# Prompt value products in groups of eight score blocks, the sample's over pairs of page tiles

## The chip, the cores and the metric

The kernel runs on one core of one Trainium2 chip. The metric is the device time of one execution in microseconds (us). The engines are named as in the profile: PE is TensorE (matrix products), PEld its weight loads, DVE is VectorE, ACT ScalarE, POOL GpSimd, SP the engine that issues most transfers.

## The reference, cut to what matters

One inference step of a two-layer decoder for a prompt of 2048 tokens and for a sample batch of 8 sequences with 8 new tokens each, over 4096 cached positions. Layer one is a gated linear recurrence; layer two is attention with 16 heads of 64 over shared keys and values. Attention has a forgetting term, the difference of cumulative log forget values, and a causal mask. The sample's cached keys and values lie in pages of 128 positions, found through a page table.

```python
s = jnp.einsum('bqhd,bkhd->bhqk', q, k).astype(jnp.float32) * (HEAD_DIM ** -0.5)
s = s + jnp.swapaxes(cq, 1, 2)[:, :, :, None] - jnp.swapaxes(ck, 1, 2)[:, :, None, :]
s = jnp.where(mask[None, None], s, -jnp.inf)
p = jax.nn.softmax(s, axis=-1)
return jnp.einsum('bhqk,bkhd->bqhd', p.astype(v.dtype), v)
```

## The kernel before, in words

The recurrence layer comes first, in two chunks of the prompt, then the shared projections `k`, `v`, `q`, `g`, then prompt attention, then the output projection. The sample's attention (`decode`) is a generator that yields estimated costs; a `Side` object advances it beside the prompt's projections and attention, so the work of both stands mixed in the engines' programs. It works in 16 turns, one for a sequence and half of the heads; three turns run early (`ahead` false), the other thirteen beside the second half of the projections and beside attention (`ahead` true).

*Prompt attention* (`attention`). The work is cut into 64 units, a head and a query chunk `qc` of 512 columns; even heads go through `qc` 0 to 3, odd heads 3 to 0. A unit has 4(qc + 1) blocks of 128 keys, a head 40, all heads 640; one block is one tick. For a block, TensorE makes scores in one of two banks (`st`) with two matmuls (L1592 and L1593; on the diagonal a third, the causal mask, L1595). The contraction of 128 rows of the first holds the high and low parts of the keys (`ka`). ScalarE takes the exponential into a tile (L1601): block 0 of a unit into the unit's accumulator `acc`, the others into `p`, six buffers (NP). After every fourth block `product` is put off by two ticks. It issues the value products of the four blocks in one run with `together`: the first matmul waits for the last exponential, the others are ordered right behind it. Each product uses 64 of the 128 array columns (`ops`, L1612, `128*64`), two of them side by side for the two halves of the queries, and the trace holds two records for each. Then POOL adds the four tiles into `acc` (L108, a helper), and at the end of a unit `finish` copies the result (`oT`). After four units `total` sums the accumulators over keys (L1481), copies the sums to `cs` and stores them through SP.

The softmax maximum is a separate pass ahead of the scores: `top` makes a score block of queries against keys (`sx`, L1431) and VectorE reduces it. `advance` decides how many of these stand in each tick.

Keys and values of a head are loaded by `load_head` at the sixteenth tick of the head before: `ka`, two buffers of 2048 columns, in one transfer, and `vvt` (2048 positions by 64) in another. The low keys with the forget rows (`kbt`) and the queries have loads of their own. Loads are issued by SP, which works through its program in order; `paged` puts them behind the page load last written into the program.

*The sample* (`decode`). A page tile `raw` is four pages (128 positions by 8 heads by 64, 256 KB each) and is issued by SP (L1093). Beside attention there are four such buffers (`nraw`), taken in turn by key tiles, value tiles and two scratch tiles. A turn has eight key and eight value tiles. Key tiles are transposed on VectorE (`ktr`, L1180), which frees them, and four make a batch of scores (`dS`, L1148, `128*32`). For a value tile, `products` issues 8 matmuls, 16 records, in one run (`dO`, L1262, `128*32`, four side by side), as soon as the four pages have come; those of tile 0 are put off to the place of tile 1. The order of a period is written out by hand:

```python
for who, x in (("v", 5), ("k", 0), ("v", 6), ("k", 1), ("v", 7), ("k", 2), ("k", 3), ("v", 0), ("k", 4),
               ("v", 1), ("k", 5), ("v", 2), ("k", 6), ("v", 3), ("k", 7), ("v", 4)):
```

Here value tiles 5 to 7 belong to the turn before, and the key tiles to the next one.

*Output projection* (`project`). Seventeen row tiles, of which every other one uses lent tiles of attention: `kbt0`, one `ka` buffer (for two operands of 1024 columns) and one `vvt` tile for the output. The result of a row tile is stored whole, that of the last in halves.

Of the kernel before, what the change touches and what calls it, by code (L numbers as in the profile page):

```python
# [11 lines left out]
F32 = mybir.dt.float32  # L12
# [8 lines left out]
P = 128  # L21
# [35 lines left out]
NP = 6  # L57
# [30 lines left out]
def tile_hawk_fox(  # L88
# [954 lines left out]
    def decode(es, turns, nraw, nktr, ahead):  # L1043
# [74 lines left out]
        class Turn:  # L1118


            def __init__(self, it):
                self.b, self.hg, self.odd = *turns[it], it % 2
                self.next = turns[it + 1] if it + 1 < len(turns) else None
                self.dl, self.raws = Later(), []
# [125 lines left out]
        def values(t, xs):  # L1250
# [7 lines left out]
            def products(i, raw, came):  # L1258

                def mm(d, a):  # L1260
# [5 lines left out]
                together([partial(mm, d, a) for d in range(4) for a in range(2)], came, True)  # L1266
# [67 lines left out]
    def attention(es):  # L1334
# [46 lines left out]
        lent["psum"], lent["res"], lent["out"] = ps3, f(kbs[0][:, :]), vvs[0]  # L1381
        lent["halves"] = lambda: pool.tile([P, SEQ], F32R, name="ka", tag="ka", bufs=2)
        units = [(h, qc) for h in range(H) for qc in ((0, 1, 2, 3) if h % 2 == 0 else (3, 2, 1, 0))]
        heads, qas, mxs, oTs_, sgt = {}, {}, {}, {}, {}
# [17 lines left out]
        def load_head(h):  # L1402
            hr = slice(h * HD, (h + 1) * HD)
            ka = pool.tile([P, SEQ], F32R, name="ka", tag="ka", bufs=2)
            for lo, hi in halves(h):
                queue[0].dma_start(f(ka[:, lo:hi]), kd_d[h * HD:(h + 1) * HD, :, lo:hi].rearrange("d x t -> (d x) t"))
            queue[0].dma_start(vvs[h % 2][:, :, :], v_d[:, hr].rearrange("(k p) d -> p k d", p=P))
            heads[h] = ka
# [67 lines left out]
        def total(h2, sums, todo, single):  # L1476
# [5 lines left out]
            cs = pool.tile([P, 512], F32, name="cs", tag="cs")  # L1482
# [67 lines left out]
        load_head(0)  # L1550
# [6 lines left out]
        ops = acc = None  # L1557
        pair = []
# [10 lines left out]
        lows = [2]  # L1569

        def loads():
# [7 lines left out]
            h, k = divmod(tick, 40)  # L1579
            if k == 16 and h + 1 < H:  # L1580
                with paged():
                    load_head(h + 1)

        for u, (h, qc) in enumerate(units):
            for k in range(nks[u]):
                loads()
                ka, kb = heads[h], kbs[h % 2]
                qa, qb = qas[u], qbs[u % NQ]
                lo = max(0, k - qc * 4) * P
                ks = slice(k * P, (k + 1) * P)  # L1590
                ps = scores_bank()
# [309 lines left out]
```

## Time and profile before

| | |
|---|---|
| median of 3 runs | 3027.18 us (3025.36 to 3033.16) |
| the profiled execution's own time | 3028.43 us |
| its span, first to last instruction | 3026.4 us |
| mean granted TensorE clock | 0.969 |
| first value product of the sample beside the second half of the projections | 1404.3 us |
| first value product of the prompt | 1762.4 us |
| last value product of the sample | 2708.9 us |
| last value product of the prompt | 2823.7 us |

All places in the profile are microseconds from the start of the span. A row of the timeline has the start, the time until the end of the last instruction that it merges, engine, line, operation, tiles (output, then inputs), the array shape used, the shape of the moving operand and the number of merged records; an idle time before it stands in brackets with what ended it. Matmuls overlap in the pipeline, so the distance of two starts tells more than the length of one. A row of the waits has who waited for what, the total, the number of times and the longest.

### The profile page before, as it was taken

To read this page: it belongs to the slowest core of one execution; us is meant where nothing else is said; L and a number is where in the kernel's file an instruction comes from. 1 tells how busy PE (TensorE), PEld (TensorE's weight loads), DVE (VectorE), ACT (ScalarE), POOL (GpSimd) and SP (SyncE) were. 2 spreads that over 40 slices of the span, in tenths; PEclk is the share of its full clock that TensorE was granted. 3 is DMA by queue.
4 is the path that set the end of the run, shared out by engine and by line. 5 is a ranking of instruction groups with operands and counts; after the bars stand their busy time and mean duration, and the time that the engine had idled before them with its cause. 6 is when DMAs were issued, how large, how long until landed. Compare 5 with 4: busy or idle time off the path is not lost.

```text
span 3026.4 us, 60467 instructions
## 1 busy us (share of the span) xinstructions
PE 2803.4 (93%) x21614; PEld 2252.1 (74%) x21614; DVE 1805.5 (60%) x4012; ACT 1269.9 (42%) x2874; POOL 1084.4 (36%) x1199
## 2 busy tenths in 40 slices
PE   6998999998997999999999699998998999999998
PEld 5997789988887997888889556665665666565687
DVE  6877455425427775676564466656776756655344
ACT  4665342222125665534333234444544444355321
POOL 1653201000002653100000245665575656659422
PEclk9999999999998999999999889999999999999999
DMA  4224546888863226699999968898899888874343
GB/s 123 79 88 133 171 126 191 256 263 281 278 216 91 89 88 194 209 313 338 332 346 326 279 209 243 248 282 255 250 291 287 267 251 265 260 247 122 98 145 110
DMA packets 479103, 653.79 MB, mean 216 GB/s; under 512 B 91291, under 2 KB 277020, under 8 KB 471525
## 3 DMA queue, kind: packets, MB, share of 16 engines
q1 hardware_dynamic: 475174, 644.26, 67.4%
q10 hardware_dynamic: 3340, 3.56, 0.4%
q8 instruction: 171, 2.80, 0.4%
q0 software_dynamic: 288, 2.10, 0.2%
q14 instruction: 130, 1.06, 0.1%
HBM read 514.22 MB, written 135.16 MB: 215 GB/s over the span
## 4 chain that ended last, share of the span: by engine, by line
PE 59%; DMA 16%; DVE 9%; ACT 6%; SPq 5%; issue 3%; POOL 1%; ACTq 0%; DVEq 0%; POOLq 0%
PE ops L1612 7%; PE st L1592 4%; PE y L383 4%; PE y L384 4%; PE y L385 4%; DMA raw<-in_cache_k_dram 4%; PE sx L1431 4%; PE dO L1262 3%; DMA raw<-in_cache_v_dram 3%; PE st L1593 3%; PE dS L1148 3%; PE kv L383 3%; PE kv L385 3%; PE kv L384 3%; SPq L1093 2%
## 5 line engine op out<-in xcount | busy, mean ns | idle before, releaser
L108 POOL TENSOR_TENSOR acc<-acc,p 128x512 f32<-128x512 f32 (+3 forms) x576 | 640.9, 1114 | 347.7 <-PE ops L1612 211.2
L1601 ACT ACTIVATE p<-st 128x512 f32<-128x512 f32 (+3 forms) x576 | 291.3, 525 | 400.1 <-PE st L1593 177.5
L1180 DVE STREAM_TRANSPOSE ktr<-raw 128x1024 f32<-128x1024 f32 x256 | 308.2, 1226 | 125.1 <-DMA raw<-in_cache_k_dram 116.5
L1433 DVE TENSOR_REDUCE mxs<-sx 128x1 f32<-128x512 f32 x384 | 255.0, 681 | 141.0 <-PE sx L1431 139.6
L383 PE MATMUL kv<-wh,xh 128*128 128x256 f32 (+3 forms) x1088 | 310.0, 288 | 6.4 <-ACT wh L427 4.7
L384 PE MATMUL kv<-wl,xh 128*128 128x256 f32 (+3 forms) x1088 | 309.3, 287 | 5.7 <-DVE wl L428 5.7
L385 PE MATMUL kv<-wh,xl 128*128 128x256 f32 (+3 forms) x1088 | 309.6, 286 | 2.7 <-DMA xl<-xld 2.7
L1592 PE MATMUL st<-qa,ka 128*128 128x512 f32 (+3 forms) x640 | 269.9, 422 | 13.3 <-ACT p L1601 7.5
L1612 PE MATMUL ops<-p,vvt 128*64 128x256 f32 (+1 forms) x2176 | 262.9, 369 | 1.0 <-ACT p L1601 0.7
L1431 PE MATMUL sx<-kbt,qbt 96*128 96x512 f32 (+3 forms) x640 | 229.2, 416 | 29.9 <-DMA qbt<-qd 24.2
L1113 POOL TENSOR_TENSOR qw<-qb,amask 128x128 f32<-128x128 f32 x64 | 29.1, 460 | 618.1 <-PE dS L1148 325.3
L428 DVE SCALAR_TENSOR_TENSOR wl<-wst,gv,wh 128x256 fp32r<-128x256 f32 (+1 forms) x384 | 169.4, 504 | 131.8 <-ACT wh L427 131.5
L427 ACT ACTIVATE wh<-wst,gv 128x256 fp32r<-128x256 f32 (+1 forms) x384 | 164.6, 499 | 190.2 <-DMA wst<-in_w_kv_dram 72.7
L1593 PE MATMUL st<-qbt,kbt 128*128 128x512 f32 (+3 forms) x640 | 236.9, 370 | 0.0
L383 PE MATMUL qg<-xh,wh 128*128 128x512 f32 (+2 forms) x640 | 229.4, 359 | 0.0
L384 PE MATMUL qg<-xl,wh 128*128 128x512 f32 (+2 forms) x640 | 228.2, 357 | 0.0
L385 PE MATMUL qg<-xh,wl 128*128 128x512 f32 (+2 forms) x640 | 227.5, 356 | 0.6 <-DVE wl L428 0.6
L1612 PEld LDWEIGHTS ops<-p,vvt 128*64 128x64 f32 x2176 | 161.5, 141 | 88.2 <-issue 19.8
L383 PEld LDWEIGHTS kv<-wh,xh 128*128 128x128 f32 (+1 forms) x1088 | 203.5, 188 | 13.2 <-ACT wh L427 6.8
L384 PEld LDWEIGHTS kv<-wl,xh 128*128 128x128 f32 (+1 forms) x1088 | 203.2, 188 | 10.1 <-DVE wl L428 6.9
L385 PEld LDWEIGHTS kv<-wh,xl 128*128 128x128 f32 (+1 forms) x1088 | 204.8, 188 | 7.0 <-issue 3.7
L1592 PEld LDWEIGHTS st<-qa,ka 128*128 128x128 f32 x640 | 123.7, 193 | 112.8 <-issue 54.4
(297 smaller groups left out, 6356.3 us busy)
## 6 DMA issues: line engine op xcount, KB each, us to landing
raw<-in_cache_k_dram SPq DMA_DIRECT2D x512, 256.0 KB
raw<-in_cache_v_dram SPq DMA_DIRECT2D x512, 256.0 KB
wst<-in_w_kv_dram SPq DMA_DIRECT2D x48, 512.0 KB
wst<-in_b_w_in_dram SPq DMA_DIRECT2D x48, 512.0 KB
xt<-in_x_prompt_dram SPq DMA_DIRECT2D x32, 512.0 KB
wst<-in_a_w_in_dram SPq DMA_DIRECT2D x64, 256.0 KB
out_dram<-kf SPq DMA_DIRECT2D x128, 128.0 KB
sc<-cd SPq DMA_DIRECT2D x16, 1024.0 KB
```

The source lines that it names most:

```text
L108: eng.tensor_tensor(out, a, b, op=op)
L383: T.matmul(ps, lh(k), rh(k), start=(k == 0), stop=False)
L384: T.matmul(ps, lh(k), rl(k), start=False, stop=False)
L385: T.matmul(ps, ll(k), rh(k), start=False, stop=(k == nk - 1))
L428: V.scalar_tensor_tensor(wl[:, k, :], st[:, k, :], gk, f(wh[:, k, :]), op0=ALU.mult, op1=ALU.subtract)
L1180: behind("V", V.transpose(t.kts[pp][:, n], raw[:, :, pp * 256:(pp + 1) * 256]).ins)
L1431: T.matmul(ps[:, :w], qb[0:96, j * P:(j + 1) * P], kb[0:96, ck * 512:ck * 512 + w], start=True, stop=True)
L1433: place["V"] = V.reduce_max(mx[:, j, ck:ck + 1], ps[:, :w], axis=AX.X).ins
L1592: place["T"] = T.matmul(ps[:, lo:], ka[:, ks], qa[:, lo:], start=True, stop=False).ins
L1593: T.matmul(ps[:, lo:], kb[:, ks], qb[:, lo:], start=False, stop=(k < qc * 4))
L1601: pair.append((k, lo, p, A.activation(p[:, lo:], ps[:, lo:], AF.Exp)))
L1612: return T.matmul(ops[r * HD:(r + 1) * HD, a0 * P:], vvs[h % 2][:, k, :], p[:, :].rearrange("p (a r c) -> p a r c", a=2, r=2)[:, a0:, r, : ...
```

## The change

The prompt's value products of heads 0 to 14 are issued after every eighth block, for all eight blocks in one run, which may span two units; head 15 keeps groups of four. Block 0 goes into a `p` tile like the others, and there are ten of these. The additions into `acc` are issued right behind each exponential, the first one from blocks 0 and 1, and where block 1 covers only part of the columns POOL copies the rest from block 0. The row sums `cs` take a turn in the `p` ring and lose their own tile.

For the sample, in the thirteen later turns, the products of value tiles 0 and 1, 2 and 3, 4 and 5, 6 and 7 are issued in one run of 16 matmuls, which waits for the pages of both.

`ka` and `vvt` become three tiles each of half the length: one for the lower halves of even heads, one for those of odd heads, and one that the upper halves of all heads share. The lower halves are loaded 24 ticks ahead by SP, the upper ones early in their own head: for odd heads by ScalarE's queue, for even heads by SP.

In the output projection the lent tiles follow these halves, and each row tile's output is two tiles, stored separately.

```diff
-NP = 6
+NP = 10
+GROUP = 8
...
-            def products(i, raw, came):
-
-                def mm(d, a):
+            def products(pages_):
+
+                def mm(i, raw, d, a):
                     c = ((i + d) % 2 * 2 + a) * 32
                     return T.matmul(op[c:c + 32, :256], sx[:, d, i // 4, a * 4:(a + 1) * 4, :].rearrange("p h q -> p (h q)"),
                                     raw[:, d, a * 256:(a + 1) * 256],
                                     start=(i + d < 2), stop=(i + d == NPG - 1))
 
-                together([partial(mm, d, a) for d in range(4) for a in range(2)], came, True)
+                together([partial(mm, i, raw, d, a) for i, raw, _ in pages_ for d in range(4) for a in range(2)],
+                         [c for *_, came in pages_ for c in came], True)
...
-                dl.after(2 if ahead and x == 0 else 1, lambda i=x * 4, raw=raw, came=came: products(i, raw, came))
+                t.held.append((x * 4, raw, came))
+                if x % 2 or not ahead:
+                    dl.after(1, partial(products, t.held[:]))
+                    t.held.clear()
...
-        pool.tile([P, 512], F32, name="cs", tag="cs")
         pool.tile([P, 512], F32, name="sgt", tag="sgt", bufs=2)
-        vvs = [pool.tile([P, 16, HD], F32, name=f"vvt{i}") for i in range(2)]
-        pool.tile([P, SEQ], F32R, name="ka", tag="ka", bufs=2)
+        vvs = [pool.tile([P, 8, HD], F32, name=f"vvt{i}") for i in range(3)]
+        kas = [pool.tile([P, SEQ // 2], F32R, name=f"ka{i}") for i in range(3)]
...
-        def load_head(h):
-            hr = slice(h * HD, (h + 1) * HD)
-            ka = pool.tile([P, SEQ], F32R, name="ka", tag="ka", bufs=2)
-            for lo, hi in halves(h):
-                queue[0].dma_start(f(ka[:, lo:hi]), kd_d[h * HD:(h + 1) * HD, :, lo:hi].rearrange("d x t -> (d x) t"))
-            queue[0].dma_start(vvs[h % 2][:, :, :], v_d[:, hr].rearrange("(k p) d -> p k d", p=P))
-            heads[h] = ka
+        def place_of(h, k):
+            return h % 2 if k < 8 else 2
+
+        def load_ka(queue, h, k0, k1):
+            queue.dma_start(f(kas[place_of(h, k0)][:, k0 % 8 * P:((k1 - 1) % 8 + 1) * P]),
+                            kd_d[h * HD:(h + 1) * HD, :, k0 * P:k1 * P].rearrange("d x t -> (d x) t"))
+
+        def load_vv(queue, h, k0, k1):
+            queue.dma_start(vvs[place_of(h, k0)][:, k0 % 8:(k1 - 1) % 8 + 1, :],
+                            v_d[k0 * P:k1 * P, h * HD:(h + 1) * HD].rearrange("(k p) d -> p k d", p=P))
...
-            cs = pool.tile([P, 512], F32, name="cs", tag="cs")
+            cs = pool.tile([P, 512], F32, name="cs", tag="p", bufs=NP)
...
+        def products(todo):
+
+            def mm(u, k, lo, p, r):
+                h, qc = units[u]
+                a0 = (lo // P + 1 - r) // 2
+                return T.matmul(ops2[r * HD:(r + 1) * HD, u % 2 * 256 + a0 * P:u % 2 * 256 + 256],
+                                vvs[place_of(h, k)][:, k % 8, :],
+                                p[:, :].rearrange("p (a r c) -> p a r c", a=2, r=2)[:, a0:, r, :],
+                                start=(k == 0), stop=(k == nks[u] - 2 + r))
+
+            together([partial(mm, u, k, lo, p, r) for u, k, lo, p, _ in todo for r in range(2) if lo <= (2 + r) * P],
+                     [todo[-1][4]])
+            for u, k, *_ in todo:
+                if k == nks[u] - 1:
+                    finish(u, ops2[:, u % 2 * 256:u % 2 * 256 + 256], sums_of.pop(u))
...
+        lows, parts = [2], []
+        for h in range(1, H):
+            steps_ = [(-24, S, load_ka, 0, 8), (-24, S, load_vv, 0, 8)]
+            if h % 2:
+                steps_ += [(1, A, load_ka, 8, 12), (2, A, load_ka, 12, 16), (4, A, load_vv, 8, 16)]
+            else:
+                steps_ += [(4, S, load_ka, 8, 12), (5, S, load_vv, 8, 12), (10, S, load_ka, 12, 16), (11, S, load_vv, 12, 16)]
+            parts += [(h * 40 + t, q, fn, h, k0, k1) for t, q, fn, k0, k1 in steps_]
+        parts.sort(key=lambda x: x[0])
...
-            h, k = divmod(tick, 40)
-            if k == 16 and h + 1 < H:
-                with paged():
-                    load_head(h + 1)
+            while parts and tick >= parts[0][0]:
+                _, queue_, fn, *which = parts.pop(0)
+                with paged() if queue_ is S else ExitStack():
+                    fn(queue_, *which)
...
-                place["T"] = T.matmul(ps[:, lo:], ka[:, ks], qa[:, lo:], start=True, stop=False).ins
+                place["T"] = T.matmul(ps[:, lo:], ka[:, kx], qa[:, lo:], start=True, stop=False).ins
...
+                p = pool.tile([P, 512], F32, name="p", tag="p", bufs=NP)
+                group.append((u, k, lo, p, A.activation(p[:, lo:], ps[:, lo:], AF.Exp)))
                 if k == 0:
-                    p = acc = pool.tile([P, 512], F32, name="acc", tag="acc", bufs=NACC)
+                    first = p
+                elif k == 1:
+                    acc = sums_of[u] = pool.tile([P, 512], F32, name="acc", tag="acc", bufs=NACC)
+                    tt(a_l(), acc[:, lo:], first[:, lo:], p[:, lo:], ALU.add)
+                    if lo:
+                        cp(G, acc[:, :lo], first[:, :lo])
                 else:
-                    p = pool.tile([P, 512], F32, name="p", tag="p", bufs=NP)
-                pair.append((k, lo, p, A.activation(p[:, lo:], ps[:, lo:], AF.Exp)))
-
-                def product(u=u, h=h, todo=pair, acc=acc, last=(k == nks[u] - 1)):
-
-
-                    nonlocal ops
-                    if todo[0][0] == 0:
-                        ops = ops2[:, u % 2 * 256:u % 2 * 256 + 256]
-
-                    def mm(k, lo, p, r):
-                        a0 = (lo // P + 1 - r) // 2
-                        return T.matmul(ops[r * HD:(r + 1) * HD, a0 * P:], vvs[h % 2][:, k, :],
-                                        p[:, :].rearrange("p (a r c) -> p a r c", a=2, r=2)[:, a0:, r, :],
-                                        start=(k == 0), stop=(last and k == todo[-1][0] - 1 + r))
-
-                    together([partial(mm, k, lo, p, r) for k, lo, p, _ in todo for r in range(2) if lo <= (2 + r) * P],
-                             [todo[-1][3]])
-                    for k, lo, p, _ in todo:
-                        if k:
-                            tt(a_l(), acc[:, lo:], acc[:, lo:], p[:, lo:], ALU.add)
-                    if last:
-                        finish(u, ops, acc)
-
-                if k % 4 == 3:
-                    later.after(2, product)
-                    pair = []
+                    tt(a_l(), acc[:, lo:], acc[:, lo:], p[:, lo:], ALU.add)
+                if len(group) == (GROUP if h < H - 1 else 4):
+                    later.after(2, partial(products, group))
+                    group = []
...
-                V.scalar_tensor_tensor(y[:m, sl], yps[j][:m, :], r[:m, 0:1], bpostB[:m, sl], op0=ALU.mult, op1=ALU.mult)
-                tt(V if i == len(rows) - 1 and j == 1 else G, y[:m, sl], y[:m, sl], x1[:m, sl], ALU.add)
-                if i == len(rows) - 1:
-                    S.dma_start(dst[:, sl], y[:m, sl])
-            if i < len(rows) - 1:
-                S.dma_start(dst, y[:m, :])
+                V.scalar_tensor_tensor(y[j][:m, :], yps[j][:m, :], r[:m, 0:1], bpostB[:m, sl], op0=ALU.mult, op1=ALU.mult)
+                tt(V if i == len(rows) - 1 and j == 1 else G, y[j][:m, :], y[j][:m, :], x1[:m, sl], ALU.add)
+                S.dma_start(dst[:, sl], y[j][:m, :])
...
-                dict(og=tiled(lent["res"][:, :D]), x1=lent["res"][:, D:], oh=tiled(hs[:, :D]), ol=tiled(hs[:, D:]),
-                     y=lent["out"][:, :, :].rearrange("p k d -> p (k d)"),
+                dict(og=tiled(lent["res"][:, :D]), x1=lent["res"][:, D:], oh=tiled(lent["split"][0][:, :]),
+                     ol=tiled(lent["split"][1][:, :]), y=lent["out"],
```

More of the change, by code (lines that the diff above doesn't have):

```diff
@@ L1549, in attention @@
         advance(-1)
-        load_head(0)
+        for k in (0, 8):
+            load_ka(queue[0], 0, k, k + 8)
+            load_vv(queue[0], 0, k, k + 8)
         load_low(0)
@@ L1556, in attention @@
             yield 300
[L1557 to L1558 removed]
+        group, sums_of = [], {}
+        def products(todo):
[11 more added lines that the diff above has]
+                    finish(u, ops2[:, u % 2 * 256:u % 2 * 256 + 256], sums_of.pop(u))
         wide = [0]
```

16 lines of the change are left out of this document (7 added, 9 removed).

## The prediction

> **What bounds the kernel now.** I read the engine shares first, then the same shares by stage, then the waits of TensorE, then its timeline around single products.
>
> ```profile
> span 3026.4 us, 60467 instructions
> PE 2803.4 (93%) x21614; PEld 2252.1 (74%) x21614; DVE 1805.5 (60%) x4012; ACT 1269.9 (42%) x2874; POOL 1084.4 (36%) x1199
> ```
>
> TensorE leads. By stage (length, then busy time of PE, weight loads, DVE, ACT, POOL, then granted clock, DMA share, GB/s), for the three stages that the change touches:
>
> ```profile
> 1300.00:1730.00 430.00, 404.96 (x3725) 349.94 (x3723) 255.37 (x500) 153.77 (x397) 24.36 (x45) 0.98 0.99 328
> 1762.00:2710.00 948.00, 891.98 (x8168) 569.90 (x8167) 618.68 (x1311) 429.24 (x1063) 585.05 (x558) 0.97 0.84 260
> 2710.00:2826.00 116.00, 109.01 (x656) 68.11 (x655) 60.45 (x112) 69.14 (x147) 101.04 (x84) 1.00 0.40 118
> ```
>
> The first is shared projections with the sample beside them, the second prompt attention with the sample beside it, the third prompt attention alone. In each TensorE is busy 94% of the time, no other engine is (POOL comes near in the short third), and DMA is full only in the first. So a stretch of TensorE time that disappears should mostly shorten the run. What is in it?
>
> ```profile
> PEld st L1592 <- issue: 53.6, 166, 0.8
> PEld dO L1262 <- issue: 36.9, 57, 3.4
> PEld ops L1612 <- issue: 26.2, 95, 0.7
> PEld st L1592 <- ACT p L1601: 37.6, 87, 1.7
> PE st L1592 <- ACT p L1601: 7.5, 20, 0.8
> PEld ops L1612 <- ACT p L1601: 27.3, 64, 2.2
> PE ops L1612 <- ACT p L1601: 4.1, 7, 2.0
> PE dO L1262 <- DMA raw<-in_cache_v_dram: 19.4, 13, 3.1
> ```
>
> These are TensorE's waits in prompt attention (total us, times, longest). The first three name no releaser: the weight load sits idle without waiting for anything shown, and it does so at the first score (`st`) after something, at the sample's value products (`dO`) and at the prompt's (`ops`). The count of the first, 166, is about that of the runs of products. The timeline shows why:
>
> ```profile
> 2682.31 0.40 PE L1592 MATMUL st<-qa,ka 128*128 128x512 f32 x1
> 2682.54 0.40 PE L1593 MATMUL st<-qbt,kbt 128*128 128x512 f32 x1
> 2682.87 2.80 PE L1262 MATMUL dO<-raw,sx 128*32 128x256 f32 x48
> 2685.60 0.50 PE L1592 MATMUL st<-qa,ka 128*128 128x512 f32 x1
> 2685.93 0.39 PE L1593 MATMUL st<-qbt,kbt 128*128 128x512 f32 x1
> 2686.16 0.57 PE L1431 MATMUL sx<-kbt,qbt 96*128 96x384 f32 x2
> ...
> 2522.59 1.07 PE L1262 MATMUL dO<-raw,sx 128*32 128x256 f32 x16 [0.33 <-DMA raw<-in_cache_v_dram]
> 2523.59 0.91 PE L1431 MATMUL sx<-kbt,qbt 96*128 96x512 f32 x3
> ...
> 2525.91 1.95 PE L1612 MATMUL ops<-p,vvt 128*64 128x256 f32 x16
> 2527.78 0.50 PE L1592 MATMUL st<-qa,ka 128*128 128x512 f32 x1
> 2528.12 0.39 PE L1593 MATMUL st<-qbt,kbt 128*128 128x512 f32 x1
> 2528.35 0.39 PE L1431 MATMUL sx<-kbt,qbt 96*128 96x512 f32 x1
> ```
>
> Go by start times. A full 128x512 matmul follows another after 0.23 us (2682.31 to 2682.54). The narrow run after it starts 0.33 later: 0.10 extra on entry. After the run the first score takes 0.33 (2685.60 to 2685.93), then the pace is 0.23 again: 0.10 extra behind it. The run itself: 48 records last 2.73 us from start to next start, 16 last 1.00, so another 16 cost (2.73 - 1.00) / 2 = 0.865 and each run pays 0.135 once. A separate run of narrow products thus costs **0.335 us** more than the same products appended to another. `ops` shows the same: 2527.78 to 2528.12 is 0.34, again 0.10 over.
>
> **The change, part by part.**
>
> *Fewer prompt runs.* Heads 0 to 14 have 15 x 40 = 600 score blocks: 150 groups of four become 75 of eight; head 15 keeps fours. 75 x 0.335 = **25.1 us** less. The 0.135 inside is measured on `dO`; no pair of `ops` runs shows it. Bounds: 0.20 (entry and exit alone, 15.0 us) and 0.335; I take 0.335, the same kind of matmul being the nearest row.
>
> *Fewer sample runs.* Thirteen turns of eight page tiles are 104 runs; in the second stage the timeline has three x32 (the first is below) and the x48 above, five runs joined already, so 99.
>
> ```profile
> 1883.57 1.93 PE L1262 MATMUL dO<-raw,sx 128*32 128x256 f32 x32
> ```
> ```profile
> 1300.00:1730.00 430.00, 24.60 (x368) 9.84 (x368) 0.98 0.99 328
> ```
>
> Pairs make 52: 47 x 0.335 = **15.7 us** less, by the lower bound 9.4. The second row, of `dO` alone, puts 368 records, 23 tiles, into the first stage: some eleven of the 47, under a DMA share of 0.99. TensorE is 94% busy there too; I count them.
>
> *Longer score runs between products.* Only two score banks exist, so the third score must wait for the first one's exponential. Behind products both banks are free; then two of four blocks can wait, and in groups of eight six of eight. Today's waits on exponentials are 37.6 + 7.5 = 45.1 us. At half as much again: +22.6. The other end is 0.
>
> ```profile
> L1601 ACT ACTIVATE p<-st 128x512 f32<-128x512 f32 x384 | 221.5, 596 | 237.8 <-PE st L1593 177.5 <-POOL acc L108 25.5 <-PE st L1595 19.5
> L1431 PE MATMUL sx<-kbt,qbt 96*128 96x512 f32 (+3 forms) x640 | 229.2, 416 | 29.9 <-DMA qbt<-qd 24.2
> ```
>
> An exponential takes 0.596 us. A full block is two matmuls of 0.23, and there are as many row-maximum matmuls (640) as blocks, so about 0.7 us of TensorE per block without the sample's work. ScalarE keeps up on average; nearer to 0. I take **+8**.
>
> *Entry waits.* Products wait for their last exponential: 27.3 + 4.1 = 31.4 us at 71 entries. Half the entries: between 0 and -15; I take **-5**, because the wait may just move to the scores.
>
> *Sums on POOL.* The adds now come right after each exponential instead of behind the products, the first block goes through `p`, and 16 copies of 128x128 are new.
>
> ```profile
> ACT p L1601 <- POOL acc L108: 38.1, 34, 3.5
> L108 POOL TENSOR_TENSOR acc<-acc,p 128x128 f32<-128x128 f32 x64 | 32.1, 501 | 9.5 <-ACT p L1601 5.7
> ```
>
> The copies are 16 x about 0.5 = 8 us. They and the earlier adds now stand ahead of the gate products and query masks on POOL, which is busy 585 of 948 us: hidden; were POOL full, 8. ScalarE's 38.1 us of waiting for buffers should go: with ten buffers, the tenth block behind a group's first needs a buffer whose product stands ahead of that score on TensorE anyway. On the path between 0 and -15; I take 0. The row-sum tile now takes a turn in the same ring; it needs its store to leave within ten blocks, some 16 us: 0.
>
> *Keys and values in halves.* The same bytes; the upper halves of all heads share one tile. A block takes (948 + 116) / 640 = 1.66 us. For even heads they go through SP 16 blocks or more ahead of use; nothing waits. For odd heads three loads each, 24 in all, are issued by ScalarE between exponentials, the first seven blocks, some 11 us, ahead of use.
>
> ```profile
> L1406 ACTq DMA_DIRECT2D ka<-kd x2: 349/396/442, 1738.3 to 1738.7; - x2
> 1739.67 5.79 ACTq L1419 DMA_DIRECT2D qa<-qd  x2
> ```
>
> 24 x 0.4 = 10 us of ScalarE, queued ahead of exponentials for which TensorE waits; on the path 0 to 10, and were each to stall like the second row, 24 x 2.9 = 70. That row is from the opening, eleven loads in a row; here one stands alone. I take **+3**.
>
> *Page tiles held longer.* There are four `raw` buffers. An even value tile is now freed with the odd one. Walking the ring of a turn, only the fifth value tile's load comes to wait for something later: for the products of tiles 2 and 3, not of 2. SP issues and uses, one turn:
>
> ```profile
> 2521.86 0.33 SPq L1093 DMA_DIRECT2D raw<-in_cache_v_dram  x1
> 2525.51 1.92 SPq L1093 DMA_DIRECT2D raw<-in_cache_v_dram  x4
> ...
> 2529.71 1.07 PE L1262 MATMUL dO<-raw,sx 128*32 128x256 f32 x16 [0.49 <-issue]
> 2537.96 1.07 PE L1262 MATMUL dO<-raw,sx 128*32 128x256 f32 x16
> ```
>
> The fifth tile was issued at 2521.86 and used at 2529.71. It would be issued once the product that started at 2522.59 (shown above) and its new partner end, about 2524.5, and be used with the sixth at 2537.96: 13.4 us for two tiles, against 7.9 for one. In return an even tile no longer stops TensorE by itself, so of the 19.4 us of page waits some go; the joined run waits for two tiles, and every score behind it on TensorE waits with it. Bounds -10 and +40 (the third rival); I take **+4**.
>
> *Given back.* A shorter TensorE meets transfers of fixed length sooner (the row-sum round trip, query loads): **+4**. The output stage stores halves, 16 stores more at about 0.4 us of an idle SP: 0.
>
> Sum: -25.1 - 15.7 + 8 - 5 + 3 + 4 + 4 = **-26.8 us**. The profiled execution took 3028.4 us (span 3026.4 and 2.0 around it), 1.2 above the median of 3027.2. So 3028.4 - 26.8 = 3001.6, or 3000.4 by the median: I say **3001**. Its own range: no new score waits (-8) and all entry waits gone (-10 more) give 2984; the high end of the score waits (+14.6) gives 3016.
>
> The Trainium skill, "Perfetto Trace Analysis", section "Identifying the Most-Contended Engine", speaks against all this: it holds matmul busy time to be a poor measure and asks for the share of weight loads. By that the second stage is at 60% (569.90 of 948), and the time would come nearer to the first rival's. The trace agrees in part: the 0.50 of the first score behind a run, against 0.39, counts as busy.
>
> **The rivals.**
>
> *The time comes back as waits.* The lower switch price, 122 x 0.20 = 24.4, with the other terms as in the sum (+14) gives -10; with score runs paced by exponentials to the high end (+22.6 for +8) it gives +4: 3018 to 3033. For it: two banks, 107 waits already. Against: ScalarE is busy 45% of the stage, and its commonest wait is for TensorE.
>
> *The page stream falls behind (slower).* Place: the even value tiles in their buffers. If two tiles need longer than the 13.4 us between the two products, TensorE stands still there. One tile had 7.9 us and just sufficed; two one after the other would be 15.8, 2.4 late. SP, held at that place, would bring the next pair as late: 26 x 2.4 = 62 us, less 27: **3064**. It decides from 13.4 us for two tiles. Against it: the tiles overlap in flight, and the stage moves 260 GB/s where the first reached 328.
>
> *The shared upper half comes late.* Eight odd heads each wait if 256 KB takes over 11 us from ScalarE's queue: at 16 us, 8 x 5 = 40, less 27: 3042. For it: one buffer, nothing in the trace shows that queue in mid-stage. The Trainium skill, "DMA: Bandwidth & Descriptors", section "Queues, rings and completion order", has each DMA engine take turns between queues packet by packet, so this load would not stand behind SP's pages; by that this rival is next to nothing. No row here shows it.
>
> *The runs are not joined.* Were other work put into them, nothing would change: 3027. Every group in the timelines shown is contiguous, and the code orders each behind its first matmul. Next to nothing.
>
> **How the numbers follow.** Forecast 0.69 (2984 to 3016); waits 0.14; page stream 0.11; upper half 0.05; not joined 0.01. The range for 8 in 10 reaches from 2984 over the first rival to 3033; it leaves out most of the other rivals and a little below. A measurement here tells about 0.3%, 9 us, from no change: faster is below 3018, slower above 3036. The forecast lies below; of the waits 0.04 below and 0.10 within; a milder page stream (0.01) and unjoined runs within; the rest above: faster 0.73, same 0.12, slower 0.15.
>
> **What would show it.** The changed profile should have about 75 fewer `ops` runs, most of 32 records and about 3.6 us (1.87 + 16 records without the fixed part), `dO` runs of 32 at about 1.87 us, and the first three idle rows cut by a third to a half. Score waits on exponentials should rise by less than 20 us, ScalarE's waits for POOL should nearly vanish. A `dO` wait for pages of 40 us or more, or idle time at the ninth block of odd heads, would mean the rivals; an `ops` run of 32 near 3.74 us would mean that 0.135 is no fixed price.

## The result, and the profile after

The changed kernel takes **3104.65 us** (median, 3101.79 to 3105.97) against 3028.04 of the kernel before on the same chip: a ratio of 1.0247, 95% interval 1.0229 to 1.0265. It is slower by some 77 us; the prediction said 27 faster.

First the page of the changed kernel, and its busy time by stage with the columns of the prediction's second fence.

```profile
span 3104.1 us, 60544 instructions
PE 2820.2 (91%) x21614; PEld 2283.5 (74%) x21614; DVE 1799.3 (58%) x4012; ACT 1265.0 (41%) x2874; POOL 1083.4 (35%) x1215
...
1300.00:1730.00 430.00, 398.70 (x3695) 349.30 (x3693) 251.61 (x497) 153.44 (x397) 18.73 (x37) 0.97 0.97 324
1762.00:2710.00 948.00, 848.12 (x7637) 556.41 (x7635) 584.34 (x1219) 393.01 (x977) 547.26 (x534) 0.92 0.79 242
```

The first stage is as before; the joined sample runs there, 11 of the 47 that the prediction counted, show no gain that can be told (the prompt's first value product comes 0.8 us earlier). In the second, TensorE gets 7637 matmul records done in the same 948 us instead of 8168, and its granted clock falls from 0.97 to 0.92. The first product of the prompt comes at 1761.6 us (before 1762.4), the last at 2949.1 (before 2871.4): all 78 us are lost in prompt attention. (The 2823.7 in the table ahead of the prediction is that of the last product ahead of the output projection; head 15's last ones stand among the first output rows.)

TensorE's waits from 1762 to 2900 us, for rows that the prediction spoke of and for four new ones; two rows of the kernel before stand behind them:

```profile
PEld st L1626 <- issue: 31.9, 88, 0.8
...
PEld st L1626 <- ACT p L1632: 53.4, 115, 7.0
PE st L1626 <- ACT p L1632: 20.3, 34, 6.6
PEld ops L1573 <- ACT p L1632: 30.3, 33, 10.3
PE ops L1573 <- ACT p L1632: 17.0, 11, 9.9
PE dO L1263 <- DMA raw<-in_cache_v_dram: 7.5, 2, 6.5
...
PEld mps L1455 <- DVE mrow L1451: 27.3, 17, 4.8
PE mps L1455 <- DVE mrow L1451: 22.7, 12, 4.6
PEld sx L1438 <- DVE mxs L1440: 27.1, 38, 3.2
PEld sx L1438 <- DVE mxs L1442: 17.9, 19, 3.1
```
```profile
PEld mps L1448 <- DVE mrow L1444: 3.8, 4, 1.6
PE mps L1448 <- DVE mrow L1444: 6.1, 5, 3.4
```

The joined runs are there: the first row had 53.6 us and 166 times before. The page waits fell too (19.4 to 7.5). What rose are waits of the softmax maximum: for `mrow`, the row of maxima that is transposed (`mps`), and for the reductions `mxs` (8.5 and 6.5 before on PEld). The two rows of the scores (`st`) and those of the products (`ops`) are not to be added: all 20.3 us of the first PE row lie within the 53.4 of its PEld row, all 17.0 of the second within the 30.3. In the rest of a PEld row matmuls are still running.

One such place, TensorE first:

```profile
2212.12 0.48 PE L1626 MATMUL st<-qa,ka 128*128 128x512 f32 x1
2212.44 0.39 PE L1627 MATMUL st<-qbt,kbt 128*128 128x512 f32 x1
2212.67 1.15 PE L1438 MATMUL sx<-kbt,qbt 96*128 96x512 f32 x3
2214.86 1.20 PE L1438 MATMUL sx<-kbt,qbt 96*128 96x512 f32 x3 [1.03 <-DVE mxs L1440]
2219.57 1.94 PE L1488 MATMUL tot<-acc,ones 128*32 128x512 f32 x8 [3.52 <-DVE mxs L1440]
2221.25 3.61 PE L1149 MATMUL dS<-ktr,qw 128*32 128x128 f32 x64
2224.79 0.96 PE L1438 MATMUL sx<-kbt,qbt 96*128 96x512 f32 x3
2225.59 0.40 PE L1626 MATMUL st<-qa,ka 128*128 128x512 f32 x1
```

ScalarE and VectorE in the same stretch:

```profile
2212.05 1.11 ACT L1457 ACTIVATE qbt<-mps,less 4x128 fp32r<-4x128 f32 x4
2221.62 0.59 ACT L1491 COPY cs<-tot 128x512 f32<-128x512 f32 x1 [8.46 <-PE tot L1488]
2222.11 0.77 ACT L1632 ACTIVATE p<-st 128x128 f32<-128x128 f32 x2
```
```profile
2214.93 0.69 DVE L1440 TENSOR_REDUCE mxs<-sx 128x1 f32<-128x512 f32 x1
2218.14 0.71 DVE L1159 STREAM_TRANSPOSE sy<-rawn 128x512 f32<-128x512 f32 x1 [2.52 <-DMA rawn<-ksd]
```

Between 2212.44 and 2225.59 TensorE makes no score: nine row maxima (`sx`), the row sums (`tot`) and sample work only. ScalarE stands 8.46 us at the copy of the row sums, with two finished scores in the banks whose exponentials are written behind that copy. So when VectorE halts 2.5 us for a transfer of the sample, TensorE has nothing else to do.

### The profile page after: what moved, and what is told of

It is laid out like the page before. It is cut to its first block, busy times and chain, and to the rows that moved or that the text cites. A ratio compares the mean times of both kernels' runs of the same rounds, so it can differ in the third digit from the quotient of the medians.

```text
span 3104.1 us, 60544 instructions
## 1 busy us (share of the span) xinstructions
PE 2820.2 (91%) x21614; PEld 2283.5 (74%) x21614; DVE 1799.3 (58%) x4012; ACT 1265.0 (41%) x2874; POOL 1083.4 (35%) x1215
## 4 chain that ended last, share of the span: by engine, by line
PE 44%; DMA 20%; DVE 8%; SPq 4%; ACT 4%; issue 3%; POOL 1%; ACTq 0%; DVEq 0%; POOLq 0%
PE ops L1573 6%; DMA raw<-in_cache_k_dram 6%; PE st L1626 3%; PE dO L1263 3%; PE sx L1438 3%; PE y L385 3%; PE y L384 3%; PE y L386 3%; PE dS L1149 3%; PE st L1627 2%; SPq L1094 2%; DMA raw<-in_cache_v_dram 2%; DVE ktr L1181 2%; DMA sc<-cd 2%; PE qg L384 2%
## 5 line engine op out<-in xcount | busy, mean ns | idle before, releaser
L109 POOL TENSOR_TENSOR acc<-acc,p 128x512 f32<-128x512 f32 (+3 forms) x512 | 558.7, 1092 | 268.4 <-ACT p L1632 237.9
L1632 ACT ACTIVATE p<-st 128x512 f32<-128x512 f32 (+3 forms) x640 | 321.7, 533 | 391.9 <-PE st L1627 209.0
L1573 PE MATMUL ops<-p,vvt 128*64 128x256 f32 (+1 forms) x2432 | 282.1, 375 | 17.1 <-ACT p L1632 17.0
L1626 PE MATMUL st<-qa,ka 128*128 128x512 f32 (+3 forms) x640 | 270.3, 423 | 26.9 <-ACT p L1632 20.3
L1438 PE MATMUL sx<-kbt,qbt 96*128 96x512 f32 (+3 forms) x640 | 240.2, 435 | 53.6 <-DMA qbt<-qd 24.4
L1573 PEld LDWEIGHTS ops<-p,vvt 128*64 128x64 f32 x2432 | 185.9, 142 | 106.8 <-ACT p L1632 30.3
L1438 PEld LDWEIGHTS sx<-kbt,qbt 96*128 96x128 f32 x640 | 122.0, 207 | 127.0 <-issue 47.1
```

The source lines that it names most:

```text
L109: eng.tensor_tensor(out, a, b, op=op)
L1438: T.matmul(ps[:, :w], qb[0:96, j * P:(j + 1) * P], kb[0:96, ck * 512:ck * 512 + w], start=True, stop=True)
L1573: return T.matmul(ops2[r * HD:(r + 1) * HD, u % 2 * 256 + a0 * P:u % 2 * 256 + 256], vvs[place_of(h, k)][:, k % 8, :], p[:, :].rearrange(" ...
L1626: place["T"] = T.matmul(ps[:, lo:], ka[:, kx], qa[:, lo:], start=True, stop=False).ins
L1632: group.append((u, k, lo, p, A.activation(p[:, lo:], ps[:, lo:], AF.Exp)))
```

## The experiments

Each ratio is to the kernel before, measured beside it on the same chip, with its 95% interval; a ratio of 1.01 is 30 us. Where two changed kernels are compared, each stands by its own ratio, and both intervals count. Theories A, B and C of the first batch: ScalarE's loads hold its exponentials; the page pairs do it; the groups of eight do it.

**First batch: one part undone or alone.** `e1_sp_loads`, the changed kernel with the odd heads' upper halves loaded by SP:

```diff
-                steps_ += [(1, A, load_ka, 8, 12), (2, A, load_ka, 12, 16), (4, A, load_vv, 8, 16)]
+                steps_ += [(1, S, load_ka, 8, 12), (2, S, load_ka, 12, 16), (4, S, load_vv, 8, 16)]
```

> The changed kernel, with the three upper-half loads of each odd head issued by SP at the same ticks instead of by ScalarE. Theory A (ScalarE is held at its own transfers, whose issue waits for others to land): the five holds of 1.9 to 11.2 us go, about 30 us of ScalarE, and with the half-clock stretches behind them 20 to 40 us of the 77: 3065 to 3085. Theory B (held page tiles make key pages late, VectorE stands at them and the row maxima come late): 3095 to 3110. Theory C (score runs of eight are paced by the exponentials): 3095 to 3110.

Measured 3097.5, 1.0222 (1.0195 to 1.0249): A falls. No exponential waits for a transfer any more (29.7 us in the changed kernel), and the intervals of the two ratios overlap. `e2_groups_of_4`, the changed kernel with `GROUP = 4`:

> The changed kernel with groups of four in every head; halves, ten buffers, early additions and sample pairs stay. Theory C: the loss was in the runs of eight, so the time falls to 3025 to 3050 although 75 runs come back. Theories A and B: the loss stays and the 75 runs cost up to 25 us more: 3105 to 3130.

Measured 3083.6, 1.0191 (1.0169 to 1.0214): C falls as the main cause. The time lies in none of the ranges given. `e3_no_pairs`, the changed kernel with the old call for the sample's products, and `e4_pairs_only`, the kernel before with the pairs:

```diff
-                t.held.append((x * 4, raw, came))
-                if x % 2 or not ahead:
-                    dl.after(1, partial(products, t.held[:]))
-                    t.held.clear()
+                dl.after(2 if ahead and x == 0 else 1, partial(products, [(x * 4, raw, came)]))
```

> The changed kernel with the sample's products again one run for each page tile. Theory B: the late key pages go, 40 us or more come back in spite of 47 more runs (16 us): 3040 to 3065. Theories A and C: 16 us more: 3110 to 3125.

> The kernel before with the sample's pairs alone. Theory B: slower than before by 30 us or more, 3055 and up. Theories A and C: the 47 runs saved show, 10 to 16 us faster than before: 3012 to 3020.

Measured 3090.0, 1.0197 (1.0175 to 1.022), and 3047.5, 1.0055 (1.0035 to 1.0076). Both lie between the ranges that the theories gave. The pairs cost something, but not the loss: all three theories were wrong.

**Second batch: the other parts, and the pages.** `e5_early_sums` is the kernel before with block 0 in `p` and the additions right behind the exponentials (groups of four, six buffers), `e6_halves_only` the kernel before with keys, values and output in halves, ScalarE's loads included. `s1` and `s2` load 64 of each page's 512 columns (and, not shown in the cut, take their four page tiles in turn by hand and zero them once).

```diff
-                d = S.dma_start(raw[:, i, :], page.rearrange("o k h d -> (o k) (h d)"))
+                w_ = 64 if ahead else 512
+                d = S.dma_start(raw[:, i, :w_], page.rearrange("o k h d -> (o k) (h d)")[:, :w_])
```

> The kernel before with one part of the change: block 0 goes into a p tile and POOL's additions are issued right behind each exponential; groups of four, six buffers, whole key and value tiles, no sample pairs. If the part is neutral, as the prediction had it: within 9 us of before. If POOL's place in the order matters (its gate products and query masks now stand behind additions that wait for exponentials): 20 us or more slower.

> The kernel before with the other part: key and value tiles in halves, with ScalarE's queue for odd heads, and the output stored in halves; groups of four, sums as before, no sample pairs. Theory A (transfers): 20 to 40 us slower than before, with holds of ScalarE at its own loads. If the part is neutral: within 9 us.

> The kernel before, where beside attention each page load brings only 64 of 512 columns (the sample's results from the rest are left out); buffers, waits and instructions stay. The reference for the next one. If pages bound the stage at all: 2960 to 3010; if not, 3015 to 3025.

> The changed kernel with the same short page loads. Theory B (late pages, VectorE behind them): the loss is gone and the joined runs show, 20 to 40 us faster than the short-page kernel before. Theories A and C (ScalarE's holds, exponentials): still 20 us or more slower than it.

Measured 1.0028 (1.0004 to 1.0051), 1.0007 (0.9981 to 1.0032), 0.9951 (0.9931 to 0.9971) and 1.0131 (1.0088 to 1.0174). With short pages the changed kernel is still 1.8% above the original one, so pages explain about a quarter of the loss at most. In the kernel before they are worth 0.5%, 13 us, a little less than was named for the case that they bound the stage at all. `e5` and `e6` are neutral, within the 9 us named for that.

**Third batch: the row sums.** What no kernel had undone was the row-sum tile `cs`, which takes a turn in the ring of `p`. `f1_own_row_sum_tile` gives it a tile of its own; for the space there are nine buffers:

```diff
-NP = 10
+NP = 9
...
-            cs = pool.tile([P, 512], F32, name="cs", tag="p", bufs=NP)
+            cs = pool.tile([P, 512], F32, name="cs", tag="cs")
```

> The changed kernel with a tile of its own for the row sums, as before, and nine exponential buffers instead of ten. Three theories are left. Ring: the row-sum tile in the exponentials' ring (its copy, its store and the next exponential wait for one another) costs some 30 us; then this is 3065 to 3080. Bursts: the groups of eight make the helpers late and the clock gate doubles the gaps; then this stays at 3095 to 3110. Scatter: any small change moves the queues' order and with it the time by tens of us; then it can land anywhere between 3060 and 3110, and the small edit of the original kernel sent with it moves by 10 us or more too.

Measured **1.0003** (0.9987 to 1.0019): the loss is gone with these two lines, far below the range of any of the three theories. `f2_sum_of_parts` (own tile, six buffers, `GROUP = 4`, the rest changed) and `f3_groups_of_4_no_pairs` (`cs` still in the ring):

> The original kernel with three parts of the change at once, each of which was measured alone: pairs of page tiles (+17 of the other kernel with groups of four, whose time this is compared with), early sums (+8), halves (0); groups of four, six buffers, row-sum tile of its own. If the parts add up: 3045 to 3058. Ring: the same, since the ring's new tenant and the ten buffers are what it lacks against the kernel with groups of four (3084). Bursts, with pairs and early sums worsening each other: 3070 to 3090.

> The changed kernel with groups of four and without the pairs: what is left is ten buffers, the row-sum tile in their ring, early sums and halves. Ring: 3055 to 3075. Parts add up without the ring: 3030 to 3045. Its distance to the changed kernel without pairs (3090) is the price of the groups of eight alone: bursts say +20 to +45 us, the prediction said -22.

Measured 1.0023 (1.0 to 1.0045) and 1.0129 (1.0106 to 1.0152). The first misses its expectation (3045 to 3058, measured 3032.9): the parts don't add up once the turn in the ring is gone. The second lies in the range of the ring. So with the turn in the ring, groups of four and no pairs, about half of the loss is left, and groups of eight are then some 21 us slower than groups of four (e3 against f3); the prediction had them 22 faster.

`n1_order_only` sizes a change of mere order in the kernel before:

```diff
-                later.after(3, lambda: gate(qc, sg))
+                later.after(4, lambda: gate(qc, sg))
```

> The original kernel with one number changed: a gate product goes out four blocks behind its load instead of three, 64 instructions in the whole kernel, the same work. It sizes what a mere change of order does. Bursts and ring: within 5 us of the kernel before. Scatter: 10 us or more to either side.

Measured 1.0031 (1.0016 to 1.0046). An edit without work moves this kernel by 9 us, between the two ranges expected; a part's price of that size can't be told from a shuffled order.

**Fourth batch: the turn in the ring or the number of buffers.** `g1_sums_in_acc_ten` keeps ten buffers and copies the row sums into an accumulator that they were made from:

```diff
-            cs = pool.tile([P, 512], F32, name="cs", tag="p", bufs=NP)
+            cs = todo[-1][1]
```

> The changed kernel with all ten exponential buffers, and the row sums copied into the last of the accumulators that they were made from, so that no tile of theirs takes a turn among the exponentials. Ring (the turn costs; the number of buffers does not): 3020 to 3035, and the stretches of row maxima without a score behind the row sums (9 in a row, up to 13 us, some 104 us over the attention) fall back to about 55 us. If it were the ten buffers: 3090 to 3110.

Measured 0.9995 (0.9973 to 1.0018). `g5_ring_alone` makes the turn alone in the kernel before (`cs` in the ring of `p`, `NP = 7`):

> The original kernel with this one part of the change: the row-sum tile takes a turn in the ring of the exponential buffers, of which there are then seven; nothing else. Ring: slower by 25 to 80 us (3050 to 3105), with stretches of five to nine row maxima without a score behind the row sums, which the kernel before does not have. Rival, that the turn only costs with groups of eight or with the early sums: within 10 us of the kernel before.

Measured **1.0258** (1.0219 to 1.0296): the whole loss without any other part of the change. Here is its TensorE behind the first head, then that of g1:

```profile
1830.45 0.39 PE L1592 MATMUL st<-qbt,kbt 128*128 128x512 f32 x1
1830.68 0.63 PE L1430 MATMUL sx<-kbt,qbt 96*128 96x512 f32 x2
...
1835.16 0.47 PE L1447 MATMUL mps<-ident,mrow 128*128 128x128 f32 x1 [3.33 <-DVE mrow L1443]
1835.56 1.94 PE L1480 MATMUL tot<-acc,ones 128*32 128x512 f32 x8
1837.43 1.42 PE L1430 MATMUL sx<-kbt,qbt 96*128 96x512 f32 x2
1839.01 1.29 PE L1430 MATMUL sx<-kbt,qbt 96*128 96x512 f32 x2 [0.16 <-DVE mxs L1432]
1840.60 1.54 PE L1430 MATMUL sx<-kbt,qbt 96*128 96x512 f32 x3 [0.30 <-DVE mxs L1432]
...
1845.42 0.50 PE L1591 MATMUL st<-qa,ka 128*128 128x512 f32 x1
```
```profile
1833.20 0.39 PE L1626 MATMUL st<-qa,ka 128*128 128x512 f32 x1
1833.43 0.39 PE L1627 MATMUL st<-qbt,kbt 128*128 128x512 f32 x1
1833.66 0.27 PE L1455 MATMUL mps<-ident,mrow 128*128 128x128 f32 x1
1833.86 1.06 PE L1488 MATMUL tot<-acc,ones 128*32 128x512 f32 x8
1834.85 0.50 PE L1438 MATMUL sx<-kbt,qbt 96*128 96x512 f32 x1
1835.86 0.41 PE L1227 MATMUL dsum<-ddg,ones 128*128 128x64 f32 x2 [0.51 <-DVE ddg L109]
1836.08 0.48 PE L1626 MATMUL st<-qa,ka 128*128 128x512 f32 x1
```

With the ring there are 15.0 us from one score to the next, without it 2.6. `g2_own_no_pairs` (f1 with the old call for the sample's products) and `g3_own_no_pairs_sp` (that with e1's edit):

> The changed kernel with a row-sum tile of its own, nine buffers and without the pairs of page tiles: groups of eight, halves and early sums stay. By the parts (pairs +17): 3005 to 3015. If the parts do not add up once the ring is gone: 3020 to 3035.

> As the kernel beside it (own row-sum tile, nine buffers, no pairs), and the upper halves of the odd heads are loaded by SP instead of ScalarE. By the parts (ScalarE's holds 7 us): 2998 to 3010, faster than the kernel before by 0.5 to 0.9%. If the holds lie beside other waits: the same as its neighbour within 4 us.

Measured 1.0095 (1.0058 to 1.0131) and 1.0082 (1.0053 to 1.0111). Both expectations miss: without the pairs this kernel is slower, not faster.

**Fifth batch: order or buffer.** The trace gives the number of exponentials that ScalarE has done when it comes to each copy of row sums:

```
before  49  89 133 170 213 250 286 327 ...
f1      51  89 131 173 213 252 289 331 ...
after   43  83 123 163 203 243 283 323 ...
g5      43  84 123 164 203 244 283 324 ...
```

In the two kernels with the ring three or four exponentials of the next head go ahead of the copy, every time. In the other two, 6 to 13 exponentials of the next head go first in the places listed. `i1_order_of_copy_alone` lays that order on the kernel before, with its own tile and six buffers:

```diff
-            A.copy(cs[rows, :], ps[rows, :])
+            place["A"] = A.copy(cs[rows, :], ps[rows, :]).ins
...
-                pair.append((k, lo, p, A.activation(p[:, lo:], ps[:, lo:], AF.Exp)))
+                ex = A.activation(p[:, lo:], ps[:, lo:], AF.Exp)
+                behind("A", ex.ins)
+                pair.append((k, lo, p, ex))
```

> The original kernel, row-sum tile of its own and six buffers as there, with an order laid on ScalarE's queue and nothing else: each exponential that the program writes behind a copy of the row sums also stands behind it on ScalarE. In the program so made the copies come after 43, 83, 123, 163, ... exponentials, as in the changed kernel, instead of 49, 89, 133, 170, ... If the order is what costs: 3075 to 3105, with the stretches of row maxima behind the row sums. If it is the shared buffer and its store: 3020 to 3035.

Measured **1.0211** (1.0187 to 1.0234). The order alone, without a shared buffer, makes 2.1 of the 2.6% that the turn in the ring makes in the same kernel (g5). The intervals overlap, so the rest, some 14 us, may be the buffer or chance. Its stage and its waits look like those of the changed kernel:

```profile
1762.00:2710.00 948.00, 866.24 (x7789) 550.03 (x7787) 596.93 (x1256) 405.49 (x1010) 554.68 (x532) 0.94 0.80 248
...
PEld mps L1448 <- DVE mrow L1444: 30.1, 11, 8.3
PE mps L1448 <- DVE mrow L1444: 26.2, 8, 8.0
```

`i2_sums_in_acc_sp_loads`, g1 with e1's edit, was tried as the best version:

> The changed kernel with the row sums out of the ring (copied into an accumulator, ten buffers) and the odd heads' upper halves loaded by SP instead of ScalarE. If the parts add up (SP instead of ScalarE was worth 7 us in the changed kernel): 3010 to 3017, faster than the kernel before by 0.3 to 0.5%. If the holds of ScalarE lie beside other waits: 3018 to 3026.

Measured 0.9993 (0.9966 to 1.0019). No version that does all the work beats the kernel before by more than can be measured.

## Why the prediction was wrong

**The step that failed** is one clause: "The row-sum tile now takes a turn in the same ring; it needs its store to leave within ten blocks, some 16 us: 0." It asked when the buffer comes free. The price lay in the order: this turn alone costs 1.0258 (g5), the order that it makes, without the shared buffer, 1.0211 (i1), 62 us. A tile with a turn among the exponentials' tiles has its place among the exponentials: the copy comes to stand in ScalarE's queue where the program writes it. Ahead of the copy lies the chain of the row sums: the last addition on POOL, `tot` on TensorE, and what TensorE's own queue holds ahead of `tot`. Until it has passed, ScalarE takes no exponential, the two score banks stay full, and the program gives TensorE row maxima instead, nine of them at 2212 us, shown above, which VectorE takes one after the other. Summed over the 14 copies of heads 0 to 13, the time from the start of the last exponential ahead of the copy to that of the first behind it is 48.0 us before, 106.6 after, 112.8 in i1 and 56.7 in g1, worked out from ScalarE's rows. It is 76.6 in g5, where part of the wait lies one place earlier: an exponential into an accumulator just ahead of the copy waits for `tot` itself (23.0 us, 4.4 before).

The idle time then costs twice. Behind the 3.33 us at 1835.16 the eight records of `tot` take 1.94 us, in g1 1.06. In the stretch of the changed kernel that corresponds to it (columns as above) the clock is

```profile
1830.00:1843.00 13.00, 7.74 (x24) 3.58 (x23) 11.51 (x30) 6.97 (x25) 3.12 (x3) 0.71 0.60 140
```

0.71, and from 1835.6 to 1845.7 it is 0.50. The Trainium skill, "TensorE: Matmul & The Clock Gate", section "HAM oscillation — how this bites in real kernels", describes it: a wait longer than a window of about 3.4 us throttles the array to half, and what follows starts cold. The trace agrees at this place, with a wait of 3.33 us. It does not always need a wait so long: of the 27 stretches at half clock in the changed kernel's prompt attention, 8 touch a wait of 3 us or more in the 3.4 us ahead of them, the others only shorter ones.

A tally of TensorE's matmul rows from the prompt's first value product to its last puts the parts together, worked out from the rows and the clock of each profiled run. "Clock" is half of the busy time that lies in stretches at half clock, "rest" the busy time without it.

| us | length | idle | clock | rest |
|---|---|---|---|---|
| before | 1109.0 | 63.0 | 26.8 | 1019.2 |
| changed | 1187.5 | 120.7 | 74.5 | 992.3 |
| i1, the order alone | 1173.9 | 98.2 | 56.8 | 1018.9 |
| g5, the ring alone | 1181.8 | 105.7 | 61.1 | 1015.0 |
| g1, the ring undone | 1105.7 | 77.0 | 38.5 | 990.2 |

With the order alone, idle time rises by 35.2 us and the clock's share by 30.0; the waits for `mrow` and `mxs` make 34.7 of the 35.2. In the changed kernel the two rise by 57.7 and 47.7, and the rest falls by 26.9.

**Fewer runs (-25.1): right; of the sample's (-15.7): too much.** Most `ops` runs have 30 or 32 records, the first idle row fell by 21.7 us, and in g1 by 34.8. In the tally's "rest", the groups of eight without the pairs (g2) save 25.1 us. The pairs take another 3.9 from g2 to g1, and 5.7 alone in the kernel before (e4), where the prediction had some 12 for this stretch. A run of 32 in g1, with the first score behind it:

```profile
1829.03 3.67 PE L1573 MATMUL ops<-p,vvt 128*64 128x256 f32 x32 [0.27 <-ACT p L1632]
1832.63 0.50 PE L1626 MATMUL st<-qa,ka 128*128 128x512 f32 x1
...
PEld st L1626 <- issue: 18.8, 54, 0.8
```

From start to start 3.60 us, as forecast.

**Longer score runs (+8, bounds 0 to +22.6): too small.** The prediction's 45.1 us of today's score waits counts the same places twice: every one of the 7.5 us of the PE row lies within the 37.6 of the PEld row. Taken by themselves, the PEld row goes from 37.6 to 53.4 in the changed kernel and 64.5 in g1, the PE row from 7.5 to 20.3 and 25.7:

```profile
PEld st L1626 <- ACT p L1632: 64.5, 121, 6.8
PE st L1626 <- ACT p L1632: 25.7, 42, 6.4
PEld ops L1573 <- ACT p L1632: 12.3, 24, 1.9
PE ops L1573 <- ACT p L1632: 3.5, 6, 1.5
```

So g1 pays +18.2 (matmuls idle) to +26.9 (weight loads idle) where +8 stood; half of 37.6 as the upper bound would be +18.8. Exponentials fill 40.5 of the 59.7 us of the PEld gaps that are longer than 0.2 us (from the rows of both engines): for the most part, eight blocks in a row come down to ScalarE's pace with two banks. The bound took today's length of at most 1.7 us; now one is 6.8 us, with ScalarE held by a transfer.

**So the forecast would have failed without the ring too.** By the tally g1 saves 29.0 us of TensorE's work, but its idle time rises by 14.0, the score waits above all, and the clock takes 11.7 more. That leaves -3.3 us in the profiled run; the ratio of g1 is 0.9995. In f1, the same kernel but for its buffers, idle time rises by 23.8 and the clock's share falls by 2.6, and the ratio is 1.0003; what sets this split is open.

**Entry waits (-5, bounds 0 to -15):** the prediction's 31.4 us also adds the two rows, of which one lies within the other. In g1 the PEld row falls from 27.3 to 12.3, but the PE row only from 4.1 to 3.5, so few of the matmuls stood idle for it. In the changed kernel they rise to 30.3 and 17.0; 9.9 of the 17.0 are one wait, at 1989.6 us, behind a ScalarE that stands 11.2 us at a load of its own.

**Sums on POOL (0): right in its rows** (ScalarE's waits for POOL 38.1 to 12.5 us); alone (e5) they cost 0.28%, within what n1 shows for no work at all.

**Halves (+3): about right.** Alone 1.0007; with the loads on SP instead the changed kernel is at 1.0222 for 1.0247, whose intervals overlap, and g1 at 0.9993 for 0.9995 (i2). No score waits for `ka` in the changed kernel: the rival of the late upper half was wrong.

**Given back (+4):** the wait of the row sums' way back (`rp` for `r`, 11.5 us on PE) did not rise, it is 5.9 in g1.

**Page tiles held longer (+4): not settled.** The page waits fell (19.4 to 7.5, and 11.9 in g1), so the rival of the page stream was wrong. But the pairs cost 0.55% alone in the kernel before, cost 0.5% in the changed one (against e3) and save 0.9% in the repaired one (f1 against g2; each by its own ratio to the kernel before). One number for the part does not exist here. Whether the order beside the scores, which the pairs shift too, decides this was not tested.

**The rivals** that had the time rise all took a wait for a transfer or an exponential. Of the true cause, a copy whose place in a queue got fixed, the prediction named the turn in the ring and priced it at nothing; the place it did not see.

## What to carry to other kernels

When a tile moves into a ring of other tiles, price its place in the queue, not only its buffer: ask which instructions now stand behind it, what it waits for, and whether the engine that feeds on them has other work. A ring saves space; an accumulator that has just been read gives the same space without an order (g1). When the parts of a change don't add up, look for the line that no experiment has undone.

## What the runs showed of the hardware

ScalarE's queue can be held by transfers that are not its own. In g1 the profile puts waits of its exponentials down to landings of page tiles that SP had issued, in the changed kernel to the sample's scratch transfers:

```profile
ACT p L1632 <- DMA raw<-in_cache_k_dram: 10.0, 3, 7.1
```
```profile
ACT p L1632 <- DMA sx<-pd: 14.2, 2, 11.2
```

In the traces the issues of SP and ScalarE together carry eight completion semaphores, each some 320 times. ScalarE's longest hold, 11.2 us to 1988.8 us, ends at a wait for two of them, and its own load is issued next, with one of the two. That an issue waits for the last transfer that used its semaphore fits this, but no run varies it. With the loads on SP (e1, i2) no exponential waits for a transfer (29.7 us in the changed kernel, 13.2 in g1), and the time does not change by more than the intervals.

And a number of order: one that no view prices. 64 gate products issued one block later, the same work, cost 0.31% (n1).
